# A hybrid decoder block: the two branch projections moved behind both tiles' token phases and made by seven products

## The chip, the core and the metric

The kernel runs on one core of one Trainium2 chip. The metric is the device time of one execution in microseconds; three runs of the kernel before gave 1926.44, 1926.42 and 1925.49, median 1926.42. The engines are named as in the profile: PE multiplies matrices (PEld is its weight load), DVE works on whole tiles elementwise, ACT evaluates functions and copies, POOL does the masking and issues one queue of transfers, SP only issues transfers (DMAs).

## The reference

One layer of a parallel-branch block on 2048 tokens with 1024 channels, all in float32 (cut to what matters):

```python
h = rms_norm(x, norm_g)
v_c, b_c, c_c, z_c, q, k, v, z_a, gate_logits = split(h @ w_in)      # 8704 columns
y_c = b_c * causal_depthwise_conv(c_c * v_c, conv_w) * silu(z_c)      # width 3
y_a = y_c @ w_conv_out
q, k = rms_norm(q, q_norm_g), rms_norm(k, k_norm_g)                   # per head of 64
o = sliding_window_attention(q, k, v, sinks) * silu(z_a)              # window 128, 16 heads, 4 kv heads
y_b = o @ w_attn_out
g_a, g_b = split(sigmoid(gate_logits + gate_b))
out = x + (g_a * y_a + g_b * y_b) @ w_out
```

## The kernel before

**Products.** A float32 operand is split into a high part (a rounding copy by ACT, `split` L241 and `two` L309) and a low part (the difference, by DVE), and a product of two operands takes three matmuls: high x high, high x low, low x high. Tokens come in two tiles of 1024, each cut into two halves of 512. A *unit* makes 256 output channels for 1024 tokens. Made plainly it needs eight products (two input halves, two output halves, two token halves), each 4 chunks x 3 = 12 matmuls of 128x128 by 128x512. Most units use Strassen-Winograd instead (`sunit`, `product` L413): seven products of sums of weights with sums of operands, whose results are combined in three PSUM banks X, V and Y. For a set of operands the sums are made once (28 tiles of 128x2x512: seven products x four chunks, all of the pool `oppool`) and serve all units that read this set; the sums of the weights are made for each unit.

The core of a Strassen unit, in the order of its products (1, 5, 6, 2, 7, 3, 4):

```python
product(xb, u, 1, ops, True);  nc.scalar.copy(Y, xb)
product(vb, u, 5, ops, True);  nc.scalar.copy(s5, vb)
product(Y, u, 6, ops, False);  add(vb, s5, Y)        # on DVE; product 7 may not start on Y before it
product(xb, u, 2, ops, False); fin(0, 0, xb)
product(Y, u, 7, ops, False);  fin(1, 1, (Y, s5))
product(vb, u, 3, ops, False); fin(0, 1, vb)
product(Y, u, 4, ops, False);  fin(1, 0, Y)
```

**Stages.** For each tile: k and v (tile 0 by token, in another form), the q units, eight cv units with four b units (the convolution), four ga and four gb units (merge gates), four z and four za units (the two SiLU gates); then the branch projections yb (attention, L1193 for the first unit and L413) and ya (convolution, `mm_t` L1156); after both tiles eight units o (the output projection, whose weights are the merged activations `mt`, and whose operand is w_out). In each tile the 32 attention steps (4 kv heads x 8 blocks: scores, exp, norm, transposition by way of DRAM, values) are laid between the products, and start once q and k are known. yb needs a new set of operands (the gated attention output) for the 28 tiles; its first unit is made by eight products in an order that needs the first operands late. ya is made wholly by eight products, on the gated convolution output split chunk by chunk (`opa`). At ya the operands of the next tile (its norm, its sums) or of w_out are formed by `next_tile` and `wo_side`.

**What sets the order.** The order of instructions is written out by hand: every product is one *tick*; `put(n, f)` lays a piece of side work behind the product of tick n, and `run` emits the side work of a tick, one piece of weight preparation (`piece`) and up to four waiting small DVE steps. Each engine executes its own instructions strictly in that order, so an instruction that waits holds all behind it on its engine; this is true of SP's queue too, which issues nearly all loads and stores. Weights are prepared about a unit ahead (a ring of 8 tiles, 4 raw tiles). L214 is the helper through which nearly all DVE instructions pass.

In the names of tiles, `wcv_sh` is the high part of a sum of weights of a cv unit, `_raw` the loaded weights, `oph` an operand of the token phase, `ophc` one of a branch, `th` a gate, `mt` the merged activations, `ocd`, `od`, `yd`, `gd` tensors in DRAM.

## Time and profile before

| | before |
|---|---|
| median of three runs | 1926.42 us |
| span of the profiled execution | 1924.4 us (the page gives no other time of that execution; the median is 2.0 more) |
| PE busy | 1914.0 us, 99% |
| DVE / ACT / POOL busy | 1511.8 / 971.8 / 579.4 us |
| DMA | 358.15 MB, mean 186 GB/s |
| chain that ended last | PE 89%, DVE 5%, DMA 2% |
| stages, us from the start | tokens of tile 0 to 730; yb 730 to 804; ya 804 to 892; tile 1 to 1606; yb to 1681; ya to 1768; o to 1924 |

The page's busy time of PE says that a matmul was in flight, not that it ran as fast as it can; how much of the time is matmul work is got by counting matmuls against the time of a stage. The groups of instructions give a mean duration; neighbours on an engine overlap a little, so that a sum of means exceeds the busy time.

### The profile page before, as it was taken

To read this page: it belongs to the slowest core of one execution; us is meant where nothing else is said; L and a number is where in the kernel's file an instruction comes from. 1 tells how busy PE (TensorE), PEld (TensorE's weight loads), DVE (VectorE), ACT (ScalarE), POOL (GpSimd) and SP (SyncE) were. 2 spreads that over 40 slices of the span, in tenths; PEclk is the share of its full clock that TensorE was granted. 3 is DMA by queue.
4 is the path that set the end of the run, shared out by engine and by line. 5 is a ranking of instruction groups with operands and counts; after the bars stand their busy time and mean duration, and the time that the engine had idled before them with its cause. 6 is when DMAs were issued, how large, how long until landed. Compare 5 with 4: busy or idle time off the path is not lost.

```text
span 1924.4 us, 27382 instructions
## 1 busy us (share of the span) xinstructions
PE 1914.0 (99%) x8774; PEld 1590.0 (83%) x8774; DVE 1511.8 (79%) x2580; ACT 971.8 (50%) x1935; POOL 579.4 (30%) x818
## 2 busy tenths in 40 slices
PE   9999999999999999999999999999999999999999
PEld 7888888888888888888878888888888888888887
DVE  7989899888878669678689888888998568755654
ACT  7655555456666444334555554556666345423221
POOL 2073435435565000011562343445564000011000
PEclk9999999999999999999999999999999999999999
DMA  8186455558787523894675554577776533786553
GB/s 306 61 240 187 151 167 169 172 171 249 240 254 231 162 97 132 300 287 84 169 202 160 165 163 141 163 225 233 239 236 217 182 110 115 261 232 131 160 174 110
DMA packets 214815, 358.15 MB, mean 186 GB/s; under 512 B 28752, under 2 KB 103504, under 8 KB 214672
## 3 DMA queue, kind: packets, MB, share of 16 engines
q1 hardware_dynamic: 180480, 272.18, 44.5%
q0 software_dynamic: 28288, 71.60, 14.8%
q10 hardware_dynamic: 5904, 12.62, 1.9%
q8 instruction: 70, 1.15, 0.3%
q14 instruction: 73, 0.60, 0.1%
HBM read 242.78 MB, written 113.51 MB: 185 GB/s over the span
## 4 chain that ended last, share of the span: by engine, by line
PE 89%; DVE 5%; DMA 2%; issue 1%; ACT 1%; POOL 1%; SPq 0%; DVEq 0%; POOLq 0%; ACTq 0%
PE Y L413 30%; PE ya L1156 9%; PE Vcv L413 4%; PE Xcv L413 4%; PE Xgb L413 2%; PE Vo L413 2%; PE Xo L413 2%; PE Vza L413 2%; PE Xza L413 2%; PE po L1018 2%; PE Vgb L413 2%; PE Vz L413 2%; PE Xz L413 2%; PE Vga L413 2%; PE Vb L413 2%; PE Xga L413 2%
## 5 line engine op out<-in xcount | busy, mean ns | idle before, releaser
L1238 POOL DMA_DIRECT2D mt<-tha x32 | 27.6, 861 | 528.1 <-DVE tha L214 513.5
L980 POOL DMA_DIRECT2D x<-fd x256 | 139.9, 553 | 119.7 <-DMA fd<-f 67.4
L953 ACT ACTIVATE p<-s,st,rq 128x128 f32<-128x128 f32 x256 | 112.9, 450 | 1.5 <-DMA fd<-f 1.4
L1001 POOL TENSOR_SCALAR_AFFINE_SELECT xh<-xh 64x512 fp32r<-64x512 f32 x64 | 66.7, 1042 | 140.2 <-DVE xl L214 101.1
L973 POOL DMA_DIRECT2D fd<-f x64 | 37.0, 577 | 229.4 <-DVE f L214 214.0
L413 PE MATMUL Xcv<-oph,wcv_ah 128*128 128x512 f32 x256 | 79.1, 390 | 0.0
L1156 PE MATMUL ya<-opa,wya_1h 128*128 128x512 f32 x256 | 78.9, 389 | 0.0
L1156 PE MATMUL ya<-opa,wya_0h 128*128 128x512 f32 x256 | 78.9, 389 | 0.0
L1001 POOL TENSOR_SCALAR_AFFINE_SELECT xl<-xl 64x512 fp32r<-64x512 f32 x64 | 63.1, 986 | 4.4
L214 DVE SCALAR_TENSOR_TENSOR tha<-tha,ya 128x512 f32<-128x512 f32 x32 | 22.0, 686 | 51.8 <-PE ya L1156 44.8
L1001 POOL TENSOR_SCALAR_AFFINE_SELECT yp<-yp 64x512 fp32r<-64x512 f32 x64 | 59.0, 921 | 4.2
L309 ACT CAST wcv_sh<-wcv_raw 128x1024 fp32r<-128x1024 f32 x16 | 16.9, 1054 | 83.8 <-DVE wcv_raw L214 83.8
L1001 POOL TENSOR_SCALAR_AFFINE_SELECT yp<-xl 64x512 fp32r<-64x512 f32 x64 | 55.9, 873 | 3.1
L1156 PEld LDWEIGHTS ya<-opa,wya_1h 128*128 128x128 f32 x256 | 48.0, 188 | 9.9
L1156 PEld LDWEIGHTS ya<-opa,wya_0h 128*128 128x128 f32 x256 | 48.0, 188 | 9.9
L214 DVE TENSOR_TENSOR o<-po,o 64x256 f32<-64x256 f32 x128 | 53.5, 418 | 3.0 <-ACT o L1030 2.1
L413 PEld LDWEIGHTS Xcv<-oph,wcv_ah 128*128 128x128 f32 x256 | 47.6, 188 | 9.6
L214 DVE SCALAR_TENSOR_TENSOR y<-u,cols,y 128x512 f32<-128x512 f32 x64 | 50.6, 790 | 3.4 <-ACT y L1067 2.2
L214 DVE TENSOR_TENSOR ophc<-zain,ophc 128x512 fp32r<-128x512 f32 x64 | 42.4, 687 | 11.1 <-ACT ophc L241 11.1
L1030 ACT COPY o<-po 64x256 f32<-64x256 f32 x128 | 47.1, 368 | 7.9 <-PE po L1018 4.2
L214 DVE TENSOR_TENSOR p<-p,st 128x512 f32<-128x512 f32 x64 | 48.3, 755 | 3.1 <-DVE st L214 0.4
L775 POOL DMA_DIRECT2D q2d<-q_h x64 | 44.2, 691 | 21.5 <-ACT q_h L770 13.0
(629 smaller groups left out, 6409.3 us busy)
## 6 DMA issues: line engine op xcount, KB each, us to landing
gd<-th SPq DMA_DIRECT2D x64, 256.0 KB, 2.9
wcv_raw<-in_w_in SPq DMA_DIRECT2D x32, 512.0 KB, 4.6
q<-q2d SPq DMA_DIRECT2D x64, 256.0 KB, 4.3
v<-vd SPq DMA_DIRECT2D x128, 128.0 KB, 3.6
fd<-f POOLq DMA_DIRECT2D x64, 256.0 KB, 4.6
x<-fd POOLq DMA_DIRECT2D x256, 64.0 KB, 3.4
wga_raw<-in_w_in SPq DMA_DIRECT2D x16, 512.0 KB, 5.0
wq_raw<-in_w_in SPq DMA_DIRECT2D x16, 512.0 KB, 4.9
```

The costliest lines, as they stand in the source:

```text
L214: r = f(*args, **kw)
L309: return (lambda: nc.scalar.copy(hi, src), lambda: vec.tensor_tensor(out=lo, in0=src, in1=hi.bitcast(F32), op=ALU.subtract))
L413: nc.tensor.matmul(ps, lhsT=w[:, j, :], rhs=b[:, m, :], start=start and j == 0 and i == 0, stop=j == KP - 1 and i == 2, skip_group_check=n ...
L775: nc.gpsimd.dma_start(q2d[t][j][half, q * 2 * HB : (q + 1) * 2 * HB, i, e, :], src[HALVES[e]].bitcast(F32).rearrange("p (b x) -> p b x", x ...
L953: nc.scalar.activation(out=p[:, i, :], in_=sg[:, i, HD : 3 * HD], func=AF.Exp, bias=st[:, 1, i : i + 1], scale=rv[:, i // 2, i % 2 : i % 2 ...
L973: nc.gpsimd.dma_start(fd, f)
L980: nc.gpsimd.dma_start(x[QUADS[k]], src[k])
L1001: nc.gpsimd.affine_select(out=d4, in_=s4, pattern=[[0, 2], [-32 * sg, 2], [0, G], [-sg, 32]], compare_op=ALU.is_gt if prev else ALU.is_ge, ...
L1018: nc.tensor.matmul(po[:, cs], lhsT=v2[:, kind, :], rhs=xx[:, :, h * HD : (h + 1) * HD], start=n == 0, stop=n == 2)
L1030: nc.scalar.copy(ov, pov[oth, :, e])
L1156: nc.tensor.matmul(ps, lhsT=w[:, j, cs], rhs=o[:, m, :], start=n == 0 and i == 0, stop=n == KC - 1 and i == 2)
L1238: nc.gpsimd.dma_start(mt[t][k, :, hs(q)], m, accum_op=ALU.add)
```

## The change

It does five things.

1. **Branch projections.** za is now made before q, its SiLU is stored (`zd`), and each attention step multiplies its output by it, so that no gating stage is left behind the token phase. The branch projections of both tiles come after the token phases of both tiles, in the order ya(0), yb(0), ya(1), yb(1), all 16 units by seven products (`mm_t`, `branch`, `yb_first` are gone); ya stores to `mt`, and yb is added to it by an accumulating DMA from POOL's queue.
2. **Paired units where the operands change.** Two units run product by product in turn (`pair`, `punit`), so that each set of four operand tiles is free after two products and can be overwritten with the following set: at z(0), za(1), z(1), every ya and yb pair, and the first two o units. All 28 operands of the following set are loaded from DRAM and split in the 24 or so ticks around the pair (`operands`).
3. **Sums of operands by way of DRAM.** The four sums of a set are made once by DVE (`four_sums`) and stored; for the attention outputs and w_out the inputs are first loaded for it (`pre_sums`). The normed operands of tile 1 are made in the same way during tile 0's za and q units (`next_tile`, `scaled_pair`).
4. **Sums of weights by way of DRAM.** For 27 units of tile 1 that use the same weights as in tile 0 the two sums are stored from ACT's queue in tile 0 (`kept`) and loaded in tile 1 (kind `D`), in place of four DVE subtractions.
5. **Smaller moves.** The norm of the probabilities goes from one DVE multiplication to four ACT copies with a scale (`att_scale`); the transpositions of the first two q units go from PE to DVE (`PE_TURNS` is empty); the row norms of tile 1 are spread by a DMA in place of PE transpositions. The table `PLACES` moves single pieces of side work by some ticks.

In counts of the built programs: PE 8776 to 8616 instructions (120 matmuls of 128x512 and 40 transpositions of 128x128 fewer), DVE 2582 to 2526, ACT 1706 to 2052 (256 more scaled copies of 128x128), POOL 820 to 820, SP 1202 to 1653 issues; the transfers add up to 494 MB, in place of 356 MB by the same count.

```diff
-PE_TURNS = ((0, 0), (0, 1))
+PE_TURNS = ()
+PLACES = {...}
+REUSED = ("q", "cv", "b", "ga", "gb", "z", "za")
+PAIR = (1, 2, 5, 6, 7, 3, 4)
+SUMS = ((0, (0, 0), (0, 1), (0, 0)), (2, (0, 1), (1, 1), (0, 1)),
+        (1, (1, 1), (1, 1), (0, 0)), (3, (1, 0), (1, 0), (1, 1)))
+LD_SUM, SUM_STEP, Z_SUM, N_SUM, N_STEP = 3, 1, 2, 6, 5
+OP_FROM, OP_STEP, OP_LD = 3, 2, 3
...
+            if kind == "D":
+                return w, [(2, 1, lambda: pair(0, 1, 2, "a")), (2, 1, lambda: pair(1, 5, 6, "s")),
+                           (2, 1, lambda: pair(2, 7, 3, "t")), (1, 1, single)]
...
+                if key[1] == 0 and key[0] in REUSED:
+                    def hi_kept():
+                        hi()
+                        to = kept[key[0], key[2], 2 - h] = dram.tile(...)
+                        nc.scalar.dma_start(to, raws[n, h])
...
+    def punit(key, fin, ops, second):
...
+        for n in PAIR:
+            product(vb if n in (5, 3) else yb if n in (6, 7, 4) else xb, u, n, ops, n in (1, 5))
...
+    def pair(a, b, ops):
+        gens = [punit(*a, ops, second=False), punit(*b, ops, second=True)]
+        for _ in PAIR:
+            for g in gens:
+                next(g)
+                yield
...
-        mul(p, p, st[:, 0].unsqueeze(2).to_broadcast([P, G, P]))
+    def att_scale(got):
+        p, st = got
+        for i in range(G):
+            nc.scalar.activation(
+                out=p[:, i, :], in_=p[:, i, :], func=AF.Copy, scale=st[:, 0, i : i + 1])
...
     def att_sum(t, j, b, got, z):
...
+        mul(o, o, z)
...
-    def mm_t(ps, u, half, opt, q, last):
...
-    def yb_first(t, ops, fin):
...
-            nc.gpsimd.dma_start(mt[t][k, :, hs(q)], m, accum_op=ALU.add)
+    def four_sums(nm, j, r, n):
...
+            sub(dst, a, b)
+            nc.sync.dma_start(d[i, j], dst)
...
+    def pre_sums(nm, j, src, n):
...
+        four_sums(nm, j, r, n + LD_SUM)
+    def operands(nm, src, n0, ops):
...
+        for k, m in enumerate(PAIR):
+            for j in range(KP):
+                n = n0 + 2 * k + OP_FROM + OP_STEP * j
+                got = []
+                put(n - OP_LD, lambda m=m, j=j, got=got: got.append(ld(m, j)), f"{nm}fl{m}.{j}")
+                put(n, lambda m=m, j=j, got=got: op_split(nm, m, j, got[0], ops), f"{nm}f{m}.{j}")
...
+            if w == 0:
+                nc.sync.dma_start(to, m)
+            else:
+                nc.gpsimd.dma_start(to, m, accum_op=ALU.add)
...
+    steps = [[74 + int(4.2 * r) for r in range(32)], [308 + int(4.5 * r) for r in range(32)]]
...
+        if t == 0:
+            next_tile(1, 24)
+            run(qunit(("ga", 0, 0), ops, fin_g(0, 0, 0)))
...
+        operands(*(("c0", ocd[0]) if t else ("h1", hd)), tick[0], following)
+        run(pair(zs[2][:2], zs[3][:2], ops))
...
+    for j in range(KP):
+        pre_sums("y1", j, od[1], tick[0] + 2 + 6 * j)
+    then = [("y0", od[0]), ("c1", ocd[1]), ("y1", od[1]), ("w", w_c)]
+    for t in range(NT):
+        for w, key in enumerate(("ya", "yb")):
+            for j in (0, 2):
...
+                if j:
+                    operands(*then.pop(0), tick[0], following)
+                run(pair(two[0][:2], two[1][:2], ops))
```

**PE, the first convolution projection of tile 0.** Before, one bank (`ya`) is finished through all eight chunks `opa` of a token half:

```order
L1156 MATMUL ya_0_0_0_8042<-opa_4_0_7939,wya_0_0l 128x512
L1156 MATMUL ya_0_0_0_8042<-opa_6_0_7942,wya_0_0h 128x512 x2
L1156 MATMUL ya_0_0_0_8042<-opa_6_0_7942,wya_0_0l 128x512
L1156 MATMUL ya_0_0_0_8042<-opa_1_0_7965,wya_0_1h 128x512 x2
L1156 MATMUL ya_0_0_0_8042<-opa_1_0_7965,wya_0_1l 128x512
```

Now, where product 1 of the pair's second unit (`Xya_1`) ends and product 2 of the first (`Xya_0`) begins:

```order
L474 MATMUL Xya_1_15255<-ophc_1_2_15017,wya_1_al 128x512
L474 MATMUL Xya_1_15255<-ophc_1_3_15072,wya_1_ah 128x512 x2
L474 MATMUL Xya_1_15255<-ophc_1_3_15072,wya_1_al 128x512
L474 MATMUL Xya_0_15220<-ophc_2_0_14974,wya_0_ah 128x512 x2
L474 MATMUL Xya_0_15220<-ophc_2_0_14974,wya_0_al 128x512
```

Products of two units alternate on the same operands; two units take 14 products, where they took 16.

**DVE, tile 0, where the last q unit gives way to the first cv unit.** Before, ahead of the sums `sl` that product 5 of cv(0) waits for:

```order
L214 SCALAR_TENSOR_TENSOR q_3_1_1_l<-q_3_1_1_t,gqk,q_3_1_1_h 128x512
L214 TENSOR_REDUCE qss_2_673<-ptq_2_1_0_1624 128x16
L214 TENSOR_TENSOR wcv_0_raw_1362<-wcv_0_raw_1362,wcv_0_raw_1364 128x512
L214 TENSOR_TENSOR wcv_0_raw_1364<-wcv_0_raw_1364 128x512
L214 TENSOR_TENSOR wcv_0_raw_1364<-wcv_0_raw_1364,wcv_0_raw_1362 128x512
L214 TENSOR_TENSOR wcv_0_raw_1362<-wcv_0_raw_1362,wcv_0_raw_1364 128x512
L214 SCALAR_TENSOR_TENSOR q_3_0_1_l<-q_3_0_1_t,gqk,q_3_0_1_h 128x512
L214 TENSOR_TENSOR wcv_0_sl<-wcv_0_raw_1364,wcv_0_sh 128x1024
```

Now, at the same place:

```order
L239 TENSOR_TENSOR st_0_1_2416<-cols,st_0_1_2416 128x4
L239 TENSOR_REDUCE qss_2_891<-ptq_2_0_1_2373 128x16
L239 SCALAR_TENSOR_TENSOR q_3_0_1_l<-q_3_0_1_t,gqk,q_3_0_1_h 128x512
L239 TENSOR_REDUCE qss_2_891<-ptq_2_1_1_2323 128x16
L239 TENSOR_TENSOR wcv_0_raw_2032<-wcv_0_raw_2032,wcv_0_raw_2053 128x512
L239 TENSOR_TENSOR wcv_0_raw_2053<-wcv_0_raw_2053 128x512
L239 TENSOR_TENSOR wcv_0_raw_2053<-wcv_0_raw_2053,wcv_0_raw_2032 128x512
L239 TENSOR_TENSOR wcv_0_raw_2032<-wcv_0_raw_2032,wcv_0_raw_2053 128x512
L239 SCALAR_TENSOR_TENSOR q_3_1_0_l<-q_3_1_0_t,gqk,q_3_1_0_h 128x512
L239 TENSOR_TENSOR st_0_1_2416<-st_0_1_2416 128x4
L239 RECIPROCAL st_0_1_2416<-st_0_1_2416 128x4
L239 TENSOR_TENSOR wcv_0_sl<-wcv_0_raw_2053,wcv_0_sh 128x1024
```

Attention steps (`st`, the statistics of a block's scores) have come in between the tail of q and the weights of cv. From the high-low difference of q(2)'s first weights to that of b(0)'s stand 199 DVE instructions, where 156 stood.

**SP, the branch projections.** Before, at yb(0): loads of chunks (`ocr`), gates (`thb`), weights and stores of `mt`:

```order
L1220 DMA mt_109<-thb_1_1_7592 128x512
L1177 DMA ocr_1_0_7729<-ocd_105 128x512
L1210 DMA thb_2_0_7731<-gd_1_112 128x512 x2
L287 DMA wya_0_raw_7749<-in_w_conv_out 128x1024
L287 DMA wya_0_raw_7751<-in_w_conv_out 128x1024
L1177 DMA ocr_3_0_7753<-ocd_105 128x512
```

Now, at the second pair of ya(0):

```order
L1363 DMA mt_111<-thy_0_2_0_0_15597 128x512
L321 DMA wyb_0_raw_15648<-in_w_attn_out 128x1024
L1297 DMA sums_y_15219<-y1r_0_0_15571 128x512
L1332 DMA y0f_2_15658<-od_103 128x512
L1363 DMA mt_111<-thy_0_3_0_0_15599 128x512
L321 DMA wyb_1_raw_15675<-in_w_attn_out 128x1024
L1297 DMA sums_y_15219<-y1r_0_1_15569 128x512
L1297 DMA sums_y_15219<-y1r_1_1_15573 128x512
L1332 DMA y0f_1_15684<-od_103 128x512
L321 DMA wyb_0_raw_15700<-in_w_attn_out 128x1024
```

Between two loads of weights now stand stores of sums, which wait for DVE, and loads of whole operands (`y0f`).

767 lines of the change are left out of this document (388 added, 379 removed), and 14 rows, old and new, of the table PLACES.

## The prediction

> **What bounds the kernel now.** I read the page's first part, then who PE waited for, then the chain that ended last.
>
> ```profile
> span 1924.4 us, 27382 instructions
> PE 1914.0 (99%) x8774; PEld 1590.0 (83%) x8774; DVE 1511.8 (79%) x2580; ACT 971.8 (50%) x1935; POOL 579.4 (30%) x818
> ```
>
> ```profile
> PE Y L1351 <- DVE zero L133: 1.5, 1, 1.5
> PE Vcv L413 <- DVE wcv_sl L214: 1.2, 3, 0.6
> PE yb L1193 <- ACT ophc L241: 0.9, 2, 0.5
> PE Vq L413 <- DVE wq_sl L214: 0.5, 1, 0.5
> PE ptr L537 <- DVE rtok L531: 0.5, 1, 0.5
> PE yb L1193 <- DVE ophc L214: 0.4, 2, 0.2
> ```
>
> PE waits for almost nothing: the two largest entries inside the program are 1.2 us (sums of cv weights) and 0.9 + 0.4 us (the change of operands at yb). So the time is PE's own work, and the first question is how much of it goes. The second is whether the others still keep up, for which I read stretches.
>
> ```profile
> core 0: us, PE busy (x) PEld busy (x) DVE busy (x) ACT busy (x) POOL busy (x), PEclk, DMA share, GB/s
> 26.00:100.00 74.00, 74.00 (x340) 61.36 (x338) 71.33 (x133) 49.73 (x89) 14.30 (x24) 1.00 0.40 129
> 100.00:200.00 100.00, 99.86 (x459) 82.01 (x458) 89.08 (x194) 54.48 (x101) 53.88 (x82) 1.00 0.74 203
> 1300.00:1400.00 100.00, 100.00 (x488) 84.57 (x487) 88.61 (x151) 66.79 (x157) 60.75 (x85) 1.00 0.76 235
> ```
>
> In the first of these stretches DVE works 71.33 of 74 us, 96%, and PE still does not wait. So DVE is nearly full in the token phase, and 96% is the highest share that I have seen it reach for long. The granted clock is 1.00 throughout, so it plays no part.
>
> **What goes.** A matmul of 512 columns is priced from the chain, in which the ya stage stands as one piece:
>
> ```profile
> 804.39 24.48 PE ya L1156 x108
> 1680.90 87.04 PE ya L1156 x384
> ```
>
> 87.04 / 384 = 0.2267 us, and 24.48 / 108 gives the same. Eight ya units go from 96 to 84 matmuls, and so do the two first yb units: 10 x 12 = 120, times 0.2267, is 27.2 us. The transpositions that leave PE:
>
> ```profile
> L628 PE MATMUL ptq<-ident,q_t 128*128 128x128 f32 x32 | 4.8, 272 | 0.0
> L537 PE MATMUL ptr<-ident,rt 128*128 128x128 f32 x8 | 1.2, 272 | 0.0
> ```
>
> 4.8 + 1.2 = 6.0 us. All of it lies on the path, since PE is the path. Together 33.2 us.
>
> **What DVE gets.** The prices:
>
> ```profile
> L214 DVE TENSOR_TENSOR p<-p,st 128x512 f32<-128x512 f32 x64 | 48.3, 755 | 3.1 <-DVE st L214 0.4
> L214 DVE TENSOR_TENSOR opa<-ocr,opa 128x512 fp32r<-128x512 f32 x32 | 20.4, 685 | 8.7 <-ACT opa L241 8.7
> L214 DVE TENSOR_TENSOR wya_0l<-wya_raw,wya_0h 128x1024 fp32r<-128x1024 f32 x8 | 9.7, 1218 | 0.0
> L214 DVE STREAM_TRANSPOSE f<-p 128x512 f32<-128x512 f32 x64 | 45.5, 711 | 3.2 <-DMA od<-o 0.2
> ```
>
> The means of all groups, times their counts, exceed the page's 1511.8 us by about 100 us over 2580 instructions, since neighbours overlap; I take 0.04 us off each. Over the program DVE gets less: 64 multiplications of p go (48.3 us), 27 x 4 subtractions of weights go (some 70 us), and sums, gating and eight more transpositions come back for about the same as the gating that goes. But the work moves. I counted the rows of DVE's order between marks and priced them so.
>
> From q(2)'s first weights to b(0)'s in tile 0 stand 199 instructions, 89.0 us, beside four units of PE with their attention, 80.6 us; before it was 156 and 73.0 us beside 77.3. Attention now begins while q is not done, four q units are transposed on DVE in place of two, and tile 1's norms and sums end there. DVE is 8.4 us short; at a 96% share 89.0 becomes 92.7, 12.1 us short. What waits behind is the addition into V after product 6, for which PE has one other product (12 x 0.2267 = 2.7 us) as cover. Ends: 0 (the weights are a unit ahead and soak it up) and 12.1; I take 8.4, since the order gives DVE no lull behind it, the next unit being 20.2 us beside 21.8.
>
> At each pair PE has 14 products, 14 x 2.72 = 38.1 us. In that time stand on DVE 53 instructions at za(1), 37.5 us; 56 at the first ya pair (six of 1024, two multiply-adds, 48 of 512), 39.6 us; 54 at the first yb pair, 38.6 us. The other pairs are under 37. So 2 us short at two pairs; at 96% it would be 0.9 + 3.1 + 2.1 = 6.1 us. The row of before that is nearest, yb's own change of operands, cost PE 0.9 + 0.4 = 1.3 us over both tiles.
>
> **What the transfers get.** The count gives 494 MB in place of 356, and before
>
> ```profile
> q1 hardware_dynamic: 180480, 272.18, 44.5%
> q0 software_dynamic: 28288, 71.60, 14.8%
> q10 hardware_dynamic: 5904, 12.62, 1.9%
> ```
>
> that took 44.5 + 14.8 + 1.9 = 61% of the 16 engines. By bytes that becomes 61 x 494/356 x 1924/1891 = 86% on average, so bursts will be over what moves. How much that is, three stretches of before show:
>
> ```profile
> 12.00:24.00 12.00, 12.00 (x55) 9.93 (x54) 7.65 (x21) 10.21 (x18) 0.00 (x0) 1.00 1.04 398
> 480.00:492.00 12.00, 12.00 (x60) 10.16 (x59) 7.75 (x14) 6.31 (x16) 9.54 (x12) 1.00 0.97 289
> 820.00:832.00 12.00, 12.00 (x57) 9.93 (x56) 5.88 (x29) 7.05 (x12) 1.69 (x2) 1.00 1.06 333
> ```
>
> With the engines full: 398 GB/s at the start (long rows), 333 at the change from tile 0 to tile 1 (tiles of 256 KB, weights), 289 amid attention (short packets). Three bursts of the new order, with a tile of 256 KB as 0.262 MB and a unit's weights as 1.05 MB:
> - tile 0, ticks 24 to 62 (103 us): rows and columns of x 8.4, spread norms 2.1, normed tiles and sums stored 7.3, weights 8.4, sums of weights stored 8.4, za stored 4.2: 38.8 MB, 376 GB/s.
> - the pair za(1) (38.1 us): the inputs and sums of od(0) 5.2, half a set of operands 3.7, tails of z 3.7, weights 2.1: about 15 MB, 390 GB/s.
> - ya(0), two pairs (76.2 us): weights 4.2, a set of operands 7.3, sums of od(1) with their inputs 8.4, gates and `mt` 8.4: 28.3 MB, 371 GB/s.
>
> At 333 they are late by 13, 6.9 and 8.8 us; at 398 by nothing; at 289 by 31, 13.8 and 21.7. I take 333, the burst that is most like them. Nothing of the first burst but weights is wanted soon, and those are loaded a unit (19 us) ahead: 0 (ends 0 and 13). The operands of the other two are loaded three ticks, 8.2 us, ahead of their split, of which landing takes about 5:
>
> ```profile
> ocr<-ocd SPq DMA_DIRECT2D x32, 256.0 KB, 4.7
> tha<-gd SPq DMA_DIRECT2D x32, 256.0 KB, 5.3
> ```
>
> So 3 us of each lateness is covered; past it a split waits at ACT and DVE, and with it their copies and additions for PE: 6.9 - 3 + 8.8 - 3 = 9.7 us. The 2 us that DVE is short at the pairs pass within these waits.
>
> The Trainium skill's page "DMA: Bandwidth & Descriptors" (Specifications) puts the HBM limit of a core at about 358 GB/s. By that the second and third burst would be late by 3.8 and 2.8 us, nearly all covered, an estimate of about 1903 for the whole. The 398 above is over that limit, so the trace does not bear it out as a ceiling.
>
> **What ACT gets.** 256 scaled copies of 128x128:
>
> ```profile
> L950 ACT ACTIVATE st<-st 128x4 f32<-128x4 f32 x64 | 13.1, 205 | 39.9 <-DVE st L214 39.6
> L241 ACT CAST opa<-ocr 128x512 fp32r<-128x512 f32 x32 | 17.6, 617 | 0.0
> L953 ACT ACTIVATE p<-s,st,rq 128x128 f32<-128x128 f32 x256 | 112.9, 450 | 1.5 <-DMA fd<-f 1.4
> ```
>
> Between 205 ns for 4 columns and 617 for 512 a straight line gives 306 ns for 128, 78 us in all, 1.2 us a step; the row for p, which reads PSUM and sums, would be the upper end, 450. Per step of attention (every 13 us) ACT rises from the 67% of 1300 to 1400 to about 76%. I cost it at nothing; its cover is that idle quarter. POOL's list is as long as before, and `mt` is accumulated by the same 32 DMAs. SP's 451 more issues, at some 0.4 us, fit beside PE at every pair (at most 52 in 38 us).
>
> **Sum.** 1924.4 - 27.2 - 6.0 + 8.4 + 9.7 = 1909.3 of span; the median of runs stood 2.0 above the span, so 1911.
>
> **Rivals.**
> - *The whole gain.* Weights a unit ahead and the margin between a split and its product hide every shortage: 1924.4 - 33.2 + 2.0 = 1893. For it speaks that DVE at 96% did not hold PE up in 26 to 100; against it that 89.0 us of work beside 80.6 cannot be hidden for four units on end.
> - *The transfers set the pace (slower).* If the bursts move at 289, as amid attention, all three hold PE up: 31 + 13.8 + 21.7 = 66.5, less 33.2: 1960. It decides from about 325 GB/s downwards, where the three sum to 33. For it: the order on SP puts stores that wait for DVE ahead of loads of weights, and the average of 86%. Against: that rate belongs to short packets, and the bursts have rows of 2 and 4 KB. That page's section "Issuing engines are not separate DMA queues" says that issuing from another engine gives no bandwidth, which would leave the stores on ACT's queue in the same contest; no run here shows it yet.
> - *ACT in the way.* If, in tile 1, every second step's scaling waits at ACT for DVE's reciprocal with PE's copies behind it, 16 x 1.2 = 19.6 us come on top: 1931. Against it is the tick that lies between reciprocal and scaling.
>
> **How the numbers follow.** The forecast 0.47; the whole gain 0.26; transfers 0.19; ACT 0.08. The forecast's own span is from 1893 to 1934 (-33.2 + 12.1 + 28.7 + 2.0 on 1924.4), which also holds the second and the fourth; leaving the transfers' case outside, the range is 1892 to 1938. No change that can be told is 0.2%, 3.9 us. Faster: 0.26 and most of 0.47, 0.71; the same 0.06; slower 0.23.
>
> **What would show it.** 7774 matmuls of 512 columns in place of 7894 at 0.227 each; ya and yb as X, V and Y banks without a stage of their own of 87 us; PE idle, or in long gaps, near q(3) and cv(0) of tile 0 for DVE, and at za(1) and ya(0) for an operand's split that waits for a DMA; DMA share over 0.9 there. I am wrong if PE waits spread over the whole token phase, or if 512-column matmuls take longer by the mean.

## The result, and the profile after

The changed kernel takes 1971.62 us (median of 4 runs, 1968.67 to 1976.70) where the kernel before took 1926.43: the ratio is 1.0236, with an interval of 1.0221 to 1.0251. It is slower by 45 us; the forecast was 1911, with a range that ended at 1938. The profiled execution took 1976.7 us, with a span of 1975.0; it is the slowest of the four, so numbers of its trace are compared with other traces, and medians with medians. Three executions of later batches that took 3206, 3371 and 7865 us are left out of every median and ratio.

The page's first parts and its DMA queues, as they were read of before:

```profile
span 1975.0 us, 28474 instructions
PE 1900.6 (96%) x8614; PEld 1569.7 (79%) x8614; DVE 1467.0 (74%) x2524; ACT 1080.0 (55%) x2267; POOL 573.0 (29%) x818
...
DMA  8489976787798779888777877798888989799553
...
DMA packets 292025, 495.88 MB, mean 251 GB/s; under 512 B 37344, under 2 KB 128480, under 8 KB 291872
...
q1 hardware_dynamic: 254512, 389.92, 61.5%
q0 software_dynamic: 28288, 71.60, 14.5%
q10 hardware_dynamic: 9072, 32.54, 4.2%
```

PE works 13 us less than before and waits 64 us more. DVE is down to 74% of the span from 79%. The transfers have gone from 358 to 496 MB and from 61% of the engines to 80%. Whom PE waited for (in total, times, longest):

```profile
PE Y L474 <- DVE Vza L239: 9.7, 2, 9.3
PE s L1042 <- DMA lows<-kd: 9.2, 2, 8.8
PE Y L474 <- DVE th L239: 8.1, 4, 6.4
PE Vza L474 <- DVE wza_sl L239: 4.7, 1, 4.7
PE Vya L474 <- DVE wya_sl L239: 4.5, 4, 1.5
PE Y L474 <- DVE q_t L239: 3.4, 3, 1.8
```

These are few and long, where before the longest inside the program was 0.6 us. To find the places, I cut the trace at the first matmul of each kind of unit. "Lost" is PE's idle time there plus what the 512-column matmuls took above 227 ns from start to start (a lowered clock shows in the second part). za0 is the stage of tile 0's za units, cv the cv and b units, ga the ga and gb units, k1 the k, v and last two za units of tile 1.

| stages | before, us | after, us | of it lost before | lost after |
|---|---|---|---|---|
| tile 0: za, q, cv, ga, z | 648.4 | 694.1 | 6.6 | 53.0 |
| tile 1: the same with k, v | 708.3 | 721.5 | 9.3 | 22.2 |
| four branch projections | 335.4 | 326.5 | 2.8 | 21.7 |
| start and o | 232.2 | 232.9 | 5.8 | 6.6 |

In sum, without the rounding of the rows, 24.3 us were lost before and 103.4 are lost after: 64 more of idle time and 15 more of matmuls that ran slow. Without the lost time the programs take 1900.1 and 1871.6 us: 28.5 us of PE's time did go, and 79 were lost for them. Four stages carry 58 of the 103 us lost; cv0 carries another 13.1 (2.4 before), in many small waits. The view of stretches (PE, PEld, DVE, ACT, POOL busy, granted clock, DMA share, GB/s) of q0 and ya0 of the kernel before, then of za0, q0, k1 and ya0 of the changed kernel:

```profile
75.65:157.87 82.22, 82.09 (x386) 67.83 (x384) 71.41 (x137) 48.97 (x79) 49.66 (x76) 1.00 0.73 196
804.23:892.20 87.97, 87.97 (x393) 72.85 (x392) 64.63 (x135) 27.82 (x44) 12.92 (x15) 1.00 0.82 233
```

```profile
75.76:170.37 94.61, 82.54 (x354) 67.00 (x352) 58.24 (x101) 44.96 (x88) 11.91 (x20) 0.95 0.90 272
170.37:268.42 98.05, 83.30 (x349) 66.76 (x348) 77.84 (x144) 49.42 (x92) 38.92 (x57) 0.93 0.91 272
810.36:904.58 94.22, 84.93 (x385) 69.74 (x384) 48.74 (x78) 35.58 (x58) 19.34 (x32) 0.95 0.81 264
1491.34:1575.45 84.11, 77.86 (x338) 62.60 (x336) 72.81 (x107) 34.26 (x53) 0.00 (x0) 1.00 0.95 339
```

The four of the changed kernel lose 16.7, 19.8, 13.7 and 7.9 us. DVE is busy 62%, 79%, 52% and 87% of them, less than the 96% at which PE did not wait before. The DMA engines are at 0.81 to 0.95, and move 264 to 339 GB/s. How a full stretch reaches PE can be followed row by row around 110 us. The timelines of SP, ACT, DVE and PE (start, duration, what, idle time before it and who ended it), and, last, the median landing of such a load in the DMA view (KB each, us from issue to landing):

```profile
100.14 4.65 SPq L1663 DMA_DIRECT2D x<-in_x  x2
```

```profile
104.02 1.05 ACT L347 CAST wza_th<-wza_raw 128x1024 fp32r<-128x1024 f32 x1
114.25 0.63 ACT L1664 ACTIVATE x<-x 128x512 f32<-128x512 f32 x1 [9.17 <-DMA x<-in_x]
...
115.65 0.58 ACT L1232 ACTIVATE th<-Xza 128x512 f32<-128x512 f32 x1
116.13 1.03 ACT L347 CAST wza_ah<-wza_raw 128x1024 fp32r<-128x1024 f32 x1
```

```profile
115.78 0.17 DVE L239 TENSOR_TENSOR msn<-ssn 128x8 f32<-128x8 f32 x1 [8.99 <-ACT x L1664]
117.19 1.22 DVE L239 TENSOR_TENSOR wza_al<-wza_raw,wza_ah 128x1024 fp32r<-128x1024 f32 x1 [1.25 <-ACT wza_ah L347]
...
119.53 0.69 DVE L239 TENSOR_TENSOR th<-Y,s5za 128x512 f32<-128x512 f32 x1
```

```profile
120.28 5.00 PE L474 MATMUL Y<-oph,wza_d 128*128 128x512 f32 x12 [6.37 <-DVE th L239]
...
141.50 2.88 PE L474 MATMUL Y<-oph,wza_d 128*128 128x512 f32 x12
```

```profile
x<-in_x SPq DMA_DIRECT2D x16, 256.0 KB, 5.8
```

The last two rows of x for tile 1's norms were issued at 100.14 and 102.16 and landed at 114.2 and 115.0, 13 to 14 us later, where the median of the 16 is 5.8. ACT stands for the first of them, with the gate of za and the next weights behind it; DVE stands for ACT's sum, with its part of the same weights and `th` behind it; PE stands 6.37 us for `th`, which holds the bank Y. Nothing of tile 1 was wanted soon, but it stood in the lists of engines that PE wants. And the gap is paid twice: the twelve matmuls behind it take 5.00 us, where the next such product takes 2.88.

### The profile page after: what moved, and what is told of

It reads as the page before. It is cut to its first block, busy times and chain, and to the rows that moved or that the text cites. A ratio compares the mean times of both kernels' runs of the same rounds, so it can differ in the third digit from the quotient of the medians.

```text
span 1975.0 us, 28474 instructions
## 1 busy us (share of the span) xinstructions
PE 1900.6 (96%) x8614; PEld 1569.7 (79%) x8614; DVE 1467.0 (74%) x2524; ACT 1080.0 (55%) x2267; POOL 573.0 (29%) x818
## 4 chain that ended last, share of the span: by engine, by line
PE 59%; DMA 8%; DVE 7%; ACT 3%; issue 2%; SPq 1%; POOL 0%; DVEq 0%; ACTq 0%; POOLq 0%
PE Y L474 21%; PE Xcv L474 3%; PE Vcv L474 3%; PE Xz L474 2%; PE Xgb L474 2%; PE Vo L474 2%; PE Xga L474 2%; PE Vgb L474 2%; PE po L1142 2%; PE Vga L474 2%; PE Vz L474 2%; DMA thy<-gd 2%; PE Xo L474 2%; PE Vb L474 1%; PE Xb L474 1%
## 5 line engine op out<-in xcount | busy, mean ns | idle before, releaser
L1366 POOL DMA_DIRECT2D mt<-thy x32 | 27.4, 860 | 353.5 <-DVE thy L239 330.3
L1085 ACT ACTIVATE p<-p,st 128x128 f32<-128x128 f32 x256 | 82.0, 393 | 20.5 <-DVE st L239 19.9
L239 DVE TENSOR_TENSOR oz<-po,oz 64x256 f32<-64x256 f32 x128 | 53.4, 417 | 9.3 <-ACT oz L1153 8.4
L1042 PE MATMUL s<-lows,kq 128*128 128x384 f32 (+2 forms) x128 | 44.8, 350 | 11.3 <-DMA lows<-kd 9.2
L1071 ACT ACTIVATION_READ_ACCUMULATOR p<-s,st,rq 128x1 f32 x256 | 50.8, 198 | 0.0
L1153 ACT COPY oz<-po 64x256 f32<-64x256 f32 x128 | 47.0, 367 | 6.6 <-PE po L1142 4.4
L239 DVE STREAM_TRANSPOSE f<-p 128x512 f32<-128x512 f32 x64 | 45.0, 704 | 6.9 <-ACT p L1085 6.1
L885 POOL DMA_DIRECT2D q2d<-q_l x64 | 44.1, 689 | 14.9 <-DMA q2d<-q_h 8.8
L1046 PEld LDWEIGHTS s<-kq,q 128*128 128x128 f32 x256 | 46.5, 192 | 1.8
L1046 PE MATMUL s<-kq,q 128*128 128x192 f32 (+2 forms) x256 | 46.7, 264 | 0.0
L239 DVE TENSOR_REDUCE st<-s 128x4 f32<-128x512 f32 x64 | 44.2, 691 | 2.0
```

Of the source, the lines that this page charges most:

```text
L239: r = f(*args, **kw)
L885: nc.gpsimd.dma_start(q2d[t][j][half, q * 2 * HB : (q + 1) * 2 * HB, i, e, :], src[HALVES[e]].bitcast(F32).rearrange("p (b x) -> p b x", x ...
L1042: nc.tensor.matmul(sp[:, h, :, skip : 3 * HD], lhsT=kq[:, 1, h * P : (h + 1) * P], rhs=kz[:, :, keys], start=True, stop=False)
L1046: nc.tensor.matmul(sp[:, h, c, skip : 3 * HD], lhsT=q2[:, h, c, :], rhs=kq[:, 0, keys], start=False, stop=c == 1)
L1071: nc.scalar.activation(out=p[:, i, :], in_=sg[:, i, HD : 3 * HD], func=AF.Exp, bias=st[:, 1, i : i + 1], scale=rv[:, i // 2, i % 2 : i % 2 ...
L1085: nc.scalar.activation(out=p[:, i, :], in_=p[:, i, :], func=AF.Copy, scale=st[:, 0, i : i + 1])
```

## The experiments

Eighteen kernels ran, each beside the kernel before on the same chip. Stages are named as above; a change of a stage is read from the profiled executions, totals from medians. The profiled execution of the changed kernel was 5 us above its median, so small differences of stages against it say little: in sums_late and norm_on_dve, which leave them nearly as they were, za0 takes 94.2 and 94.3 us for its 94.6, and q0 95.5 and 97.5 for its 98.1. One slip of the text ahead runs through some expectations: the sums of weights are kept for 31 units by 62 stores (28.4 MB less when they write an eighth), not for 27 by 54.

### Where the loss stands: four parts undone or moved

```diff
 no_kept:    -REUSED = ("q", "cv", "b", "ga", "gb", "z", "za")
             +REUSED = ()
 rows_late:  -            next_tile(1, 24)
             +            next_tile(1, 120)
 rows_late_no_kept: both
 sums_late:  -pre_sums("w", j, w_c, tick[0] + 28 + 6 * j)
             +pre_sums("w", j, w_c, tick[0] + 160 + 8 * j)
             -pre_sums("y1", j, od[1], tick[0] + 2 + 6 * j)
             +pre_sums("y1", j, od[1], tick[0] + 30 + 6 * j)
```

> Undone: the sums of weights by way of DRAM; tile 1 makes its sums on DVE again, no raw tile waits for a store, and the stretch 100 to 300 us loses the 27 x 2 stores' share of its bytes. Theory R (the rows, roots and chunks of tile 1 are loaded only three ticks ahead into a full stretch, and ACT and DVE wait for them in their order with PE's work behind): only about a fifth of the bytes of the stretch goes, so about 10 of the some 40 us lost between 100 and 300 come back: 1962, and ACT still waits 4 us or more for a load of x or h. Theory K (the kept stores hold the raw tiles, so that SP's queue stands at the next load of weights and everything behind it is late): nearly all of the 40 comes back: 1935 or less. Under both, the holes near 893 and 1500 to 1600 stay, and DVE in tile 1 rises by some 70 us without a wait for it.

> Moved: the norms and sums of tile 1 start at tick 120 (in the middle of tile 0's attention, where DMA was busy 0.7 to 0.8) in place of 24; nothing else. Theory R: the waits for x, rb, h between 100 and 300 go with it, and some 30 of the 40 us come back, of which 5 to 10 are lost again where the loads now stand: 1945. Theory K: the kept stores of za and q still hold raw tiles, but in a less full stretch; about 15 come back: 1957.

> Both of the above. Theory R: the same as the later rows alone, within 5 us: 1940 to 1945. Theory K: the same as without kept sums alone, within 5. If both are needed (bytes of the stretch alone decide): 1930, which is the sum of the two gains. What is then left over 1893 are the hole near 893 (12 us), 1500 to 1600 (13) and small waits (10).

> Moved: the loads and sums of w_out from 28 ticks into tile 1 to 160 ticks into it, and those of tile 1's attention outputs from ya(0) to yb(0), 28 ticks later. The hole near 893 (9.3 us of gap and 3 of lowered clock, where DVE waits 16.1 us for a load of w_out) goes: -12. Of the 11.1 us of gaps between 1500 and 1600 (share of DMA 0.95) two thirds go if the bytes of that stretch decide: 1971 - 12 - 8 = 1951; if the operands' short lead of three ticks decides whatever the bytes, only the first: 1959.

| | median, us | ratio to before | za0 | q0 | cv0 | k1 | q1 | cv1 | ga1 | four branches |
|---|---|---|---|---|---|---|---|---|---|---|
| after | 1971.6 | 1.0236 (1.0221 to 1.0251) | 94.6 | 98.1 | 271.8 | 94.2 | 78.7 | 256.9 | 172.7 | 326.5 |
| no_kept | 1976.2 | 1.0253 (1.0237 to 1.0269) | 84.8 | 90.5 | 271.1 | 92.6 | 83.3 | 268.2 | 172.4 | 327.3 |
| rows_late | 2003.6 | 1.0393 (1.0365 to 1.0421) | 78.0 | 84.2 | 328.0 | 91.7 | 78.7 | 257.0 | 173.5 | 326.1 |
| rows_late_no_kept | 2009.0 | 1.0427 (1.0408 to 1.0446) | 78.0 | 82.7 | 317.2 | 91.2 | 83.4 | 266.6 | 172.8 | 327.7 |
| sums_late | 1974.5 | 1.0254 (1.0226 to 1.0282) | 94.2 | 95.5 | 274.4 | 81.9 | 78.7 | 256.9 | 183.5 | 326.8 |

All four missed in their totals, and the stages say why. Without the kept sums za0 and q0 do get 17.4 us shorter, but tile 1 pays it back where DVE makes the sums again: q1 +4.6, cv1 +11.3, the first za pair (40.5 to 44.0) +3.5. So the kept sums are worth about 19 us to tile 1 and cost 17 in tile 0. With the rows of tile 1 moved, za0 falls to 78.0 and q0 by 14, so it was this work that held PE up there; but cv0, to which it moved, rises by 56. The sums of w_out leave k1 (-12, as expected) and cost 10.8 in ga1; those of y1 help yb0 and ya0 by 6.6 and cost 7.2 in ya1. The loss goes along with the transfers, wherever they are put, and nowhere gets smaller.

Theory R was right on who stands in front of PE, and wrong in that another place would be free. In rows_late the stretch at 430 shows a part of it that was not foreseen. SP's timeline and the stretch around it:

```profile
421.92 0.36 SPq L1678 DMA_DIRECT2D rd<-rtn  x1
422.37 0.53 SPq L994 DMA_DIRECT2D q<-q2d  x1
...
426.08 0.54 SPq L1025 DMA_DIRECT2D v<-vd  x1
```

```profile
420.00:430.00 10.00, 8.78 (x42) 7.06 (x41) 9.87 (x25) 5.05 (x14) 0.58 (x1) 1.00 0.27 28
430.00:440.00 10.00, 5.10 (x23) 3.90 (x21) 4.44 (x8) 3.15 (x8) 1.70 (x4) 0.94 0.74 189
```

The roots of tile 1's rows, 4 KB in 1024 elements of 4 bytes (`rd<-rtn`), landed 9.85 us after their issue; each of the loads issued between 422.37 and 426.08 landed 12 to 14 us after its own, at 436 to 438. In that time the engines were 0.27 busy and moved 28 GB/s.

### The lead, the thin transfer, and thinning out

```diff
 roots_32:   -            nc.vector.tensor_copy(rt, r)
             -            nc.sync.dma_start(rd.rearrange("b p -> p b"), rt)
             ...
             +            nc.vector.tensor_copy(rt[:, 0, :NB], r)
             +            nc.vector.transpose(out=rt[:, 1], in_=rt[:, 0])
             +            for g in range(4):
             +                nc.sync.dma_start(rd[:, 32 * g : 32 * g + 32], rt[32 * g : 32 * g + NB, 1])
 lead_6:     -LD_SUM, SUM_STEP, Z_SUM, N_SUM, N_STEP = 3, 1, 2, 6, 5
             +LD_SUM, SUM_STEP, Z_SUM, N_SUM, N_STEP = 6, 1, 2, 6, 5
 kept_from_cv_lead_4:
             +REUSED = ("cv", "b", "ga", "gb", "z")
             +OP_FROM, OP_STEP, OP_LD = 3, 2, 4
 spread:     both of kept_from_cv_lead_4, roots_32, and
             +scaled_pair(t, j, n0 + NB + LD_SUM + N_SUM + (0, 12, 24, 100)[j])
             +pre_sums("y0", j, od[0], tick[0] + 72 + 24 * j)
             +pre_sums("w", j, w_c, tick[0] + 60 + 24 * j)
             +pre_sums("y1", j, od[1], tick[0] + 2 + 14 * j)
```

> Changed: the 1024 root norms of tile 1 go to DRAM in 32 rows of 128 bytes (turned by DVE first) in place of 1024 elements of 4 bytes; nothing else. In the run with later rows the transfer of 1024 elements took 9.85 us and everything issued up to 4 us behind it landed 12 to 14 us after its issue with the DMA engines busy only 0.27. Theory S (this one transfer holds all queues): the stretch za0 (the four za units of tile 0, 94.6 us) loses the gap of 4.7 us at 152 and what its lowered clock costs, and part of those of q0 go: -8 to -12 us, so about 1962. Theory R (short lead in a full stretch, whatever that transfer): no more than 2 us: 1970.

> Changed: the loads that feed sums and norms (rows, roots, chunks of tile 1, w_out, attention outputs) are issued 6 ticks ahead of their use in place of 3, 16 us for 8. Theory R1 (the lead is short; landings took 5 to 14 us): the waits of ACT and DVE for x (9.2 us), rb and h (13), wr (16.1) go: za0 and q0 lose 15 of their 38 us of gaps and low clock, k1 12, ya0 2: 1942. Theory R2 (the bytes of the stretch decide, and an earlier issue is only an earlier place in the same queue): no more than 8 us in all, and the weights are later by it: 1963 or more.

> Changed: the sums of weights are kept only from the cv units on (not for za and q), and the operands of paired units are loaded four ticks ahead of their split in place of three. From the run without kept sums: za0 and q0 -17, since it is their own kept stores that cost there; za1, k1 and q1 +8, as their DVE work returns; cv1 stays at 256.9. The lead of operands: ya0 and yb0 lose 12.7 us above a stretch without gaps (78.4 each, less what is there without gaps); if the lead decides, half goes (-6), if the bytes, nothing. Together 1956 or 1962.

> All of the transfers thinned out: roots in 32 rows, no kept sums of za and q, operands four ticks ahead; of the pairs of chunks of tile 1 two in za0 as before, one 12 and the last 100 ticks later; sums of tile 0's attention outputs and of w_out at every 24th tick of tile 1's cv units, those of tile 1's attention outputs at every 14th in place of every 6th. By the stretches of the runs so far: za0 and q0 166 in place of 192.7 (-27), k1 -12, tile 1 +8 for its DVE sums, ya0 and yb0 -8, cv0 +10 and cv1 +5 for what stands there now: 1947. If only the bytes of each stretch decide, cv0 and cv1 take theirs without a wait: 1930. If each such load costs its wait wherever it stands: 1960.

| | median, us | ratio to before | za0 | q0 | cv0 | za1 | k1 | q1 | cv1 | four branches |
|---|---|---|---|---|---|---|---|---|---|---|
| after | 1971.6 | 1.0236 (1.0221 to 1.0251) | 94.6 | 98.1 | 271.8 | 40.5 | 94.2 | 78.7 | 256.9 | 326.5 |
| roots_32 | 1971.7 | 1.0233 (1.0216 to 1.0251) | 89.9 | 95.8 | 271.1 | 39.5 | 93.0 | 78.7 | 256.9 | 324.7 |
| lead_6 | 1974.5 | 1.0246 (1.0231 to 1.0262) | 87.8 | 110.3 | 271.9 | 39.5 | 81.9 | 80.1 | 256.9 | 330.3 |
| kept_from_cv_lead_4 | 1968.3 | 1.0208 (1.0193 to 1.0224) | 84.8 | 89.8 | 271.7 | 49.8 | 91.9 | 84.9 | 257.3 | 319.8 |
| spread | 1972.3 | 1.0232 (1.0217 to 1.0248) | 83.6 | 90.2 | 276.9 | 48.1 | 81.9 | 85.4 | 271.2 | 318.0 |

Without the 4-byte elements za0 falls by 4.7 us in the profiled executions, and q0 by 2.3, which is within what it varies by; theory S had said 8 to 12. The medians do not differ, so in total this is not shown. A lead of 16 us helps za0 (-6.8) and k1 (-12.3) and costs q0 12.2 and the branches 3.9: an earlier place in a full queue is taken from another load. That is R2, as far as the total goes. Thinning everything out gave 18.9 us in za0 and q0, 12.3 in k1 and 8.4 in the branches, and took 7.6 in za1, 6.7 in q1, 14.3 in cv1 and 5.1 in cv0. In none of the four did the total move by more than 4 us.

### The bytes by themselves

```diff
 before_more_bytes, behind each product of the kernel before:
             +            n = tick[0]
             +            nc.sync.dma_start(
             +                dram.tile([P, H], F32, name=f"more{n}"), xt2[n % KC * P : (n % KC + 1) * P, n % 4 * H : (n % 4 + 1) * H])
 before_more_issues: the same with 32 columns in place of H
```

> The kernel before, with one more transfer of 256 KB (from the input to a place in DRAM that nobody reads) issued by SP behind each of the some 680 products; no instruction waits for any of them. It brings some 170 MB, about as much as the change brings (138 MB by the same count), spread evenly. Theory B (the bytes alone: the engines are too full and all loads land late): the token phases lose as those of the changed kernel do, 30 us or more: 1957 or above. Theory L (not the bytes, but what stands in the lists: work that waits for a load of its own with a short lead, with PE's work behind it): the kernel before has leads of a unit, so no more than 8 us: 1927 to 1935.

> The control of the kernel before with 256 KB more behind each product: the same 657 issues by SP at the same places, each of 128 rows of 128 bytes (16 KB) in place of 128 rows of 2048. If the bytes made the 80 us there, nothing of them is left: 1926 to 1932. If SP's issues (657 x some 0.4 us in its list) or the number of rows made them: 1960 or more.

The kernel before with more bytes takes 2006.4 us (ratio 1.0415, 1.0400 to 1.0431), 80 us more, and with the same issues of 16 KB 1939.4 (1.0068, 1.0053 to 1.0083), 12 us more than the kernel before on that chip. The DMA packets of the two, and who PE waited for between 411 and 680 us in the first:

```profile
DMA packets 309427, 530.45 MB, mean 264 GB/s; under 512 B 39264, under 2 KB 114016, under 8 KB 309280
```

```profile
DMA packets 309427, 368.99 MB, mean 190 GB/s; under 512 B 123360, under 2 KB 198112, under 8 KB 309280
```

```profile
PE s L927 <- DMA lows<-kd: 11.4, 3, 5.8
PE Y L413 <- ACT Y L431: 6.7, 2, 5.5
PE Y L413 <- DVE zs L214: 2.2, 1, 2.2
```

Between the two, 161 MB make 67 us, and nothing waits for any of them. This is theory B, and it refutes L: the kernel before, with its leads of a unit, is not safe from bytes. They are read and written in DRAM, so at the memory the dose is twice as large: the pages count 700.8 and 377.8 MB read and written there. Where it hits is not only a matter of the share. The stages ga0, z0 and ya0, from 154.6, 83.8 and 88.0 us:

```profile
411.49:585.41 173.92, 161.21 (x751) 134.51 (x750) 128.66 (x237) 100.43 (x242) 86.19 (x122) 0.96 0.94 279
585.41:679.11 93.70, 85.97 (x391) 71.21 (x390) 65.80 (x104) 52.89 (x104) 33.12 (x44) 0.96 0.88 288
835.40:937.26 101.86, 91.93 (x393) 74.52 (x392) 64.12 (x135) 29.60 (x47) 12.93 (x15) 0.95 0.97 299
```

The stage q1 at a share of 0.95 loses nothing (80.4 for 80.0 us), nor does cv0 at 0.86 (251.5 for 251.6). PE waits in ga0 for attention's loads (`lows`, 11.4 us), in z0 for ACT's copy into Y (5.5) and in ya0 for DVE's work on the gates (`tha`, 9.6); ga1, which loses most (197.7 for 177.7), waits in small pieces for POOL, ACT and `lows`. But cv0 has 32 loads of `lows`, ga0 28, and cv0 loses nothing; so what makes a stage lose is not settled. The control loses in z0 and ya0 nearly alone, 4.5 and 6.9 us.

The same question in the changed kernel, with bytes taken away and every order and issue kept (the loads put in the place of kept sums and of sums no longer wait for the stores that made them; for the stores of sums the largest such row of SP's waits is 1.4 us):

```diff
 kept_eighth:   -                        nc.scalar.dma_start(to, raws[n, h])
                +                        nc.scalar.dma_start(to, raws[n, h][:, 0, 0])
                -                nc.sync.dma_start(raw, kept[key[0], key[2], h])
                +                nc.sync.dma_start(raw, src)
 stores_eighth: as above, and
                -            nc.sync.dma_start(d[i, j], dst)
                +            nc.sync.dma_start(d[i, j][:, : H // 8], dst[:, : H // 8])
                -                nc.sync.dma_start(h, sums_d[nm][(3, 0, 1, 2)[m - 4], j])
                +                nc.sync.dma_start(h, src[2 * j, :, hs(0)])
```

> The stores of the kept sums of weights write an eighth of their bytes (64 of 512 KB each), and tile 1 loads the plain weights in their place, as many bytes as before; so tile 1's use of them is left out of what is computed. Every instruction, wait and issue stays where it was; only 54 stores are shorter, 25 MB in all. Theory B (bytes): za0 and q0 fall as they did without kept sums (-17), and tile 1 stays as it is with them (za1 40.5, q1 78.7, cv1 256.9): 1954. Theory H (the raw tiles are held for the store and SP stands behind it, whatever the bytes): a store of 64 KB lands not much sooner, so no more than 5 us: 1966 or more.

> As the one above, and also the stores of sums of operands (96 of 256 KB) write an eighth of their bytes; the operands of products 4 to 7 are loaded from the inputs of the sums instead, as many bytes as before, so the sums themselves are left out of what is computed. 25 + 22 = 47 MB less of the 138 that the change adds, no order changed. Theory B: za0 and q0 lose another 5 of what is left there, ya0 and yb0 5: 1944. Theory H or L: within 3 us of the run above.

1952.0 us (1.0132, 1.0116 to 1.0147) and 1941.3 us (1.0069, 1.0052 to 1.0086), where theory B said 1954 and 1944. The kept stores' queue and the stages za0 and q0 of the first:

```profile
q10 hardware_dynamic: 9072, 4.10, 0.7%
```

```profile
77.30:165.94 88.64, 82.14 (x354) 66.79 (x353) 59.35 (x103) 45.92 (x89) 11.90 (x20) 0.96 0.88 263
165.94:254.09 88.15, 81.31 (x350) 65.77 (x348) 75.91 (x142) 48.78 (x92) 38.88 (x57) 0.96 0.89 251
```

28.4 MB are 19.6 us, 16 of them in za0 and q0; the next 22 MB are 10.7, which q0 (-4.3) and k1 (-2.3) show most. Theory H is not quite cut off by this run, since its shorter stores land sooner, by the median 4.0 us after their issue in za0 and q0 for 7.0. What SP waited there for them, in the changed kernel and in kept_eighth:

```profile
SPq L321 <- DMA keptwq<-wq_raw: 23.1, 4, 9.7
SPq L321 <- DMA keptwza<-wza_raw: 14.7, 3, 11.3
```

```profile
SPq L321 <- DMA keptwq<-wq_raw: 18.0, 3, 9.1
SPq L321 <- DMA keptwza<-wza_raw: 10.2, 2, 8.8
```

Three quarters of this standing are left while 16 us are gone, and no_kept, which has none of it, gained hardly more in the two stages (17.4). So little is left for H. Per MB at the engines the two steps are 0.69 and 0.49 us, and 0.42 in the kernel before (0.21 by what its memory counted). At the engines' prices the 138 MB that the change adds cost 58 to 95 us, and 29 at the lowest; the loss to be explained is 1971.6 - (1926.4 - 30.7) = 76, with the 30.7 worked out in the account of the prediction below. So the bytes can explain it, and taking away 50 of the 138 MB took back 30 us. That the others explain the remaining 46 us was not shown, since those bytes could not be taken away without their order. In stores_eighth, cv0 (12.2), za0 (10.8), k1 (9.1) and the four branches (19.7) still lose most; cv0 does not answer to these bytes at all (270.2 us for 271.8), and its loss has another cause, which stays open.

### Queues, attention and the engines

```diff
 gates_from_act:      -                nc.sync.dma_start(gd[t][w][k, :, hs(q)], th)
                      +                nc.scalar.dma_start(gd[t][w][k, :, hs(q)], th)      (zd likewise)
 attention_8_later:   -[74 + int(4.2 * r) for r in range(32)]
                      +[82 + int(4.2 * r) for r in range(32)]
 norm_on_dve:         -        for i in range(G):
                      -            nc.scalar.activation(
                      -                out=p[:, i, :], in_=p[:, i, :], func=AF.Copy, scale=st[:, 0, i : i + 1])
                      +        mul(p, p, st[:, 0].unsqueeze(2).to_broadcast([P, G, P]))
```

> Changed: the stores of the three gates (zd and gd, 96 of 256 KB) are issued by ACT, which has just made the tile, in place of SP, whose list stood 124 us in all for them. If SP's standing in front of stores delays the loads behind them, za0 loses 4 to 8 us, q0 some, the ga stages nothing (no gaps there): about 1963. If the loads are late for the bytes, nothing: 1970. ACT pays 96 x 0.35 = 34 us of issue, off the path at its 55%: at most 3 us in ga1.

> Changed: tile 0's 32 attention steps start at tick 82 (with the first cv unit) in place of 74 (with the last q unit). q0 is 98.1 us, of which 14.7 are gaps and about 4 low clock; 10.7 of the gaps are PE's waits for an attention load (8.8) and for p (1.9). If beginning attention among q is what costs there: q0 -10, cv0 and ga0 +2 together: 1963. If SP's late loads decide, the same wait stands elsewhere: 1970.

> Undone: the norm of the probabilities goes back from four ACT copies (256 of 393 ns, 82 us busy) to one multiplication on DVE (64 of about 755 ns, 48 us). If ACT stands in PE's way (PE waits for ACT's p, Y and wq_sh for 8 us in all): -4, so 1967. If DVE is short in q0 and cv0, as the prediction had it (89.0 us of work beside 80.6): +8 in tile 0, since 24 us come on top there: 1980. In tile 1 no change (cv1 has no gaps).

1982.0 us (1.0301, 1.0276 to 1.0327), 1978.8 (1.0271, 1.0256 to 1.0286) and 1981.8 (1.0283, 1.0268 to 1.0299); all three are slower than the changed kernel. With the gates' stores on ACT, za0 falls by 8.2 and q0 rises by 3.5, ga0 by 6.7, ga1 by 2.7: the loads move up and ACT pays. Over za0 and q0 together 276 GB/s move at a share of 0.90, where 272 moved at 0.90. That issuing from another engine gives no bandwidth is what the Trainium skill says in "DMA: Bandwidth & Descriptors" ("Issuing engines are not separate DMA queues"), and this trace agrees (276 for 272 GB/s). With attention later, q0 falls by 9.0 and cv0, ga0 and z0 rise by 14.0: the other of the two expectations. With the norm on DVE, cv0 takes 281.3 in place of 271.8 and tile 1 nearly the same (cv1 +1.4): DVE has no slack in tile 0's attention, as the prediction had it, though among cv and not among q.

### Parts of the change that bring no bytes, and a version from the runs

```diff
 before_turns:           -PE_TURNS = ((0, 0), (0, 1))
                         +PE_TURNS = ()
 before_turns_norm_act:  as above, and in att_norm of the kernel before, right behind the reciprocal
                         -        mul(p, p, st[:, 0].unsqueeze(2).to_broadcast([P, G, P]))
                         +        for i in range(G):
                         +            nc.scalar.activation(out=p[:, i, :], in_=p[:, i, :], func=AF.Copy, scale=st[:, 0, i : i + 1])
 rows_early: roots_32, OP_LD = 4, next_tile(1, 14), and
                         -pre_sums("w", j, w_c, tick[0] + 28 + 6 * j)       (in tile 1)
                         +pre_sums("w", j, w_c, tick[0] + 38 + 14 * j)      (from the first tick of ya0)
                         +pre_sums("y1", j, od[1], tick[0] + 2 + 14 * j)
```

> The kernel before, with one part of the change that moves no bytes: the transpositions of tile 0's first two q units go from PE to DVE (32 of 128x128 leave PE, 4.8 us by the groups; 8 of 128x512 and 711 ns come to DVE). If only the added bytes made the change slow, this part gives its full price: 1927 - 4.8 = 1922. If DVE is short among q, as the prediction had it for that place, it gives less than 1 us: 1926 or more.

> As the one above, and the norm of the probabilities by four ACT copies in place of one DVE multiplication (the other part that moves no bytes): DVE is relieved of 48 us, ACT gets some 82 us. PE does not wait for either in the kernel before, so no more than the 4.8 us: 1922; where the run above gave less for want of DVE, this one makes it up. If ACT stands in the way, 1926 or more.

> A version by what the runs showed: the rows of tile 1 ten ticks earlier (tick 14, where the DMA engines were 0.1 to 0.5 busy at 60 to 80 us), its roots in 32 rows, operands four ticks ahead, sums of w_out during yb0 and ya1 in place of k and v of tile 1, those of tile 1's attention outputs at every 14th tick. By theory B: za0 and q0 lose 15 of their 36 us as 4 MB and the following 11 move into the emptier stretch; k1 -12; ya0 and yb0 -8; ya1 +3: 1971 - 32 = 1939. If not bytes, but the waits of ACT and DVE for their own loads decide wherever they stand: start +8, za0 -4: 1962.

The transpositions alone make the kernel before 4 us slower: 1930.8 (ratio 1.0020, 1.0011 to 1.0029). The stage q0 takes 85.9 us in place of 82.2, though 32 transpositions are gone from PE, which held it for 3.0 us (not 4.8; see the next part). The first row of PE's waits in that run:

```profile
PE Y L413 <- DVE Vq L214: 4.4, 2, 3.0
```

PE waits 4.4 us for the addition into V, which stands behind the new transpositions on DVE, and 2.0 us are slower matmuls, at a granted clock of 0.98: theory "DVE is short". With the norm on ACT as well it is 1960.2 (1.0172, 1.0159 to 1.0186), with ga1 at 189.4 for 177.7 and z1 at 86.8 for 80.7. There the four copies stand in the tick of the reciprocal that they wait for, while the changed kernel puts a tick between; so this run prices ACT's standing, 29 us, and not the change's own form of it, which norm_on_dve shows to be worth 10.

The version from the runs failed: 1980.9 us (1.0284, 1.0260 to 1.0307). Its k1 (81.9) and q0 (84.5) are as good as hoped for, but za0 takes 107.9, at a DMA share of only 0.80. PE waits there 7.8 us at once for a low part of weights (`wza_tl`), which stands behind tile 1's chunks in DVE's list: for their loads, which landed 9 to 11 us after their issue, DVE stood 3.3 and 4.1 us. The rows, now among tile 0's own operands on ACT, go with two more waits of PE for a gate on ACT, 5.5 us together. No run pointed to a version that beats the kernel before.

## Why the prediction was wrong

**What goes, 33.2 us.** Right but for 4.7: without lost time the spans differ by 28.5, and the units by seven products take what was priced where no wait stands (yb0 in spread and yb1 in kept_from_cv_lead_4: 76.4 and 76.7 us, for 28 products). So the 27.2 us of matmuls came. The 6.0 of transpositions were mis-read: a group's busy time counts each matmul to its end, and the next one here starts 0.24 us before that end. In the kernel before:

```profile
95.59 0.60 PE L628 MATMUL ptq<-ident,q_t 128*128 128x128 f32 x4
95.95 0.71 PE L413 MATMUL Xq<-oph,wq_ah 128*128 128x512 f32 x2
```

Four of them hold PE for 0.36 us, and from start to start all 40 take 3.5 us: 27.2 + 3.5 = 30.7. The other 2.2 us came back in attention's small matmuls, which take 96.7 us from start to start after the change and 94.5 before.

**The step that failed** is in the part on transfers: "Nothing of the first burst but weights is wanted soon, and those are loaded a unit (19 us) ahead: 0 (ends 0 and 13)." za0 and q0 lost 36.5 us, almost three times the upper end; rows_late, which moves this work away, took 30 us from the two stages. Rows, roots and chunks of tile 1 are wanted by no product for 600 us, but ACT and DVE take them in their lists three ticks after the issue; a landing of 13 to 14 us in place of 5.8 then stands before the gates and weights that PE wants next. The same happened in k1, 13.7 us, which the sum had not at all: DVE waited there for w_out, which only the products after 1800 us want (issued at 878.78, landed 12.4 us later):

```profile
892.18 0.69 DVE L239 TENSOR_TENSOR wr<-wr,wr 128x512 f32<-128x512 f32 x1 [16.05 <-DMA wr<-in_w_out]
892.79 0.69 DVE L239 TENSOR_TENSOR Vza<-s5za,Y 128x512 f32<-128x512 f32 x1
```

The lead was held against a 5 us landing that rows of the kernel before gave, and in a full stretch that is not the landing.

**The rate.** 333 GB/s was taken and 289 set aside as belonging to short packets. za0 and q0 ran at 272 with their engines 0.9 busy; ya0 at 339. The rival "transfers set the pace" stood at 1960 and decides "from about 325 GB/s downwards": it is the one that came, 12 us beyond its price, and had a chance of 0.19. That its total is so near is partly luck: it had 35.5 us at the two later bursts, which lost 10.4, and nothing in k1, cv0 or the branches behind. The other two bursts were near: za(1) lost 2.5 us for 3.9, ya0 7.9 for 5.8; behind them yb0 and yb1 lost 5.8 each, which was not in the sum.

**DVE, 8.4 us.** A shortage at that place was not seen as such in the changed kernel: in q0 DVE was busy 79% and stood 8.2 us for loads of tile 1's chunks. That DVE has little room there, before_turns shows: 3.0 us less on PE and 8 transpositions more on DVE made the stage 3.7 us longer.

**ACT, nothing.** Not contradicted: putting the norm back on DVE costs 10 us, so ACT is the better place; that it costs nothing there is not shown by it. Its rival of 1931 was not seen in the changed kernel. That the tick between kept it out fits the run with the copies in the reciprocal's own tick, but that run is of the kernel before.

**The clock, of which the prediction said "so it plays no part".** It did, behind the waits: 15 of the 79 us.

## What to carry to other kernels

A kernel that is full on PE can be asked for its price of bytes before any rewrite: give it as many bytes that nobody waits for, with a control of as many small transfers, and read the stages that lose. Here it was 0.4 to 0.7 us per MB moved by the engines, and 138 MB for 30.7 us of PE's work is a bad trade at that price. A load is late for everyone behind its first reader in that engine's list: work that nothing needs soon still holds PE up when it stands early in the list of ACT or DVE, and what counts is the landing in that very stretch (13 us here), not the median of the program (5.8). A longer lead alone did not pay: lead_6 took 19 us from za0 and k1, and its total is 3 us longer. Fewer bytes did.
